# Twelve late modulation units: from TensorE's strips alone to TensorE's strips and VectorE in turn, with the last four placed in the output projection

## The chip, the cores and the metric

The kernel runs on one core of one Trainium2 chip. The metric is device time in microseconds (us) of one execution; the median of several executions is compared. A profile shows one execution, with each engine's instructions: TensorE (PE, matmuls; PEld, its weight loads), VectorE (DVE), ScalarE (ACT), GpSimd (POOL) and SyncE (SP, whose queue issues all loads and stores of this kernel).

## The reference, cut to what matters

Two transformer-like blocks on 256 tokens of width 2048, in fp32. The first block is modulated by a vector `c`:

```python
mod = silu(c) @ ada_w + ada_b                      # ada_w: 2048 x 12288
sh_m, sc_m, g_m, sh_f, sc_f, g_f = split(mod + ada_table, 6)
h = rms(x, norm_mix_pre) * (1 + sc_m) + sh_m
y = rwkv7_mix(h)                                   # projections, a scan over chunks, output projection w_o
x = x + g_m * rms(y, norm_mix_post)
h = rms(x, norm_ffn_pre) * (1 + sc_f) + sh_f
x = x + g_f * rms(conv_ffn(h), norm_ffn_post)
```

The second block (attention and short convolution) is not touched. What matters here is the product `silu(c) @ ada_w`: one row times a matrix of 96 MB. Of its six segments of 2048 columns, the first two (shift and scale ahead of the mixer) are wanted at once. Segments 2 (gate after the mixer), 4 (scale) and 3 (shift ahead of the feed-forward) are wanted only after the output projection, and segment 5 (gate of the feed-forward) at the end of the feed-forward.

## The kernel before, in words

*Units.* A modulation unit is 512 columns of one segment. It loads its 2048 rows as 8 tiles `raw` of 512 KB (two row blocks of 128 each) through SP's queue and adds up 16 products of a row block with 128 values of `silu(c)`. There are two ways to do that:

- `ada_group_pe` (its loads on line 250, its matmuls on line 256): TensorE multiplies a block of 32 columns, of which one holds the values, with the 512 columns. The block number modulo 4 chooses which 32 partitions of the PSUM bank are written, so four row blocks use four strips of the array. At the end ScalarE copies the bank to SBUF (line 260).
- `ada_group` (loads on line 220): VectorE multiplies the row block by a value for each partition (line 232 for the first, line 238 with the accumulator added for the other 15), into an SBUF tile `acc0`.

Either way a unit ends with its finish, `ada_fm`: four matmuls by a column of ones add up the partitions (line 273), and one or two small VectorE instructions follow (line 275 on). `ada_run` is a generator that goes through a list of units. A unit has four steps of two loads each; its finish is called `ADALAG` steps into the next unit, or with `ADALAG = 0` at the beginning of the step after its last.

*Stages.* First the value, key and low-rank projections with segments 0 and 1 (to about 295 us). Then four quarters of four head pairs each (295 to 740 us): `operands` prepares a pair, with its receptance projection `w_r` on TensorE and three stops, and between the stops the code places steps of the previous quarter's `scan` (`SSTEP` of them) and of the late units (`QSTEP` of them). The twelve late units are here: segment 2 (0 to 3), segment 4 (4 to 7), segment 3 (8 to 11), all through `ada_group_pe`, in 16 x 3 = 48 steps. A scan has a triangular inverse (lines 715 to 742, nearly all on VectorE) and then four chunks (lines 784 to 823). The last quarter's scan follows (740 to 830 us), together with a small projection `e_proj` whose evictions use the same `raw` tiles as the units; then the output projection `w_o` in four blocks of 512 columns (`tm_units`, lines 165 to 167, then `tm_out`, which evicts a block), the residual and `to_fm` (900 to 925 us), and the input of the feed-forward in 86 units of `fm_unit` (925 to 1430 us). Beside that run the four units of segment 5, written there in the code, on VectorE.

*Order.* The kernel is built with a framework whose planner lays down each engine's queue when the kernel is built. It takes what the code has earliest among what it reckons to be ready, by its own reckoning of times; the engine then runs its queue strictly in that order. Thus an instruction can stand in a queue ahead of its place in the code, as far as its tiles are free.

*Buffers.* Tiles `raw` of the units have three buffers after 295 us (`NADA2`). The accumulator `acc0` has two, in a pool `accp` that is opened in the feed-forward. The load `l2` of the low-rank weights of a pair has two.

Of the kernel before, what the change touches and what calls it, by code (L numbers as in the profile page):

```python
# [17 lines left out]
NADA = 5  # L18
NADA2 = 3

SSTEP, QSTEP = 3, 1
XL = 4
VST, WST, WP = (2, 2, 2, 2), (0, 0, 0, 0), 2
TAIL = 3
# [1 line left out]

SH = (9999, 9999)
PARTS = ((0, 25), (25, 32))
ADALAG = 2

GROUPS = ((0, 2), (2, 4), (6, 4), (10, 4), (14, 2))
P = 128
# [26 lines left out]
def body(tc, A, out):  # L59
# [5 lines left out]
    def pool(name, bufs=1, **kw):  # L65
        return tc.tile_pool(name=name, bufs=bufs, **kw)
# [146 lines left out]
    def ada_group(seg, k0, nk, accs):  # L213
# [4 lines left out]
        for q in range(KT // n):  # L218
            raw = t_(adap[0], [P, 1024], "raw").rearrange("p (a c) -> p a c", c=w_)
            SP.dma_start(raw, A["ada_w"][q * n * P:(q + 1) * n * P, c0:c0 + w_].rearrange("(a p) c -> p a c", p=P))  # L220
            for a in range(n):
                b = q * n + a
                sc = sil[:, b:b + 1]
                w = 1 if b % 4 < ada_pool[0] else 0
                if accs[w] is None:
                    accs[w] = t_(accp[0], [P, 512], f"acc{w}", bufs=2 - w)
                acc = accs[w][:, :w_]
                if first[w]:
                    if w:
                        S.activation(acc, raw[:, a, :], AF.Copy, scale=sc)  # L230
                    else:
                        V.tensor_scalar(acc, raw[:, a, :], sc, None, op0=ALU.mult)
                elif w:
                    tp = t_(small, [P, 512], "nbr", bufs=1)[:, :w_]
                    S.activation(tp, raw[:, a, :], AF.Copy, scale=sc)
                    G.tensor_tensor(acc, acc, tp, op=ALU.add)
                else:
                    V.scalar_tensor_tensor(acc, raw[:, a, :], sc, acc, op0=ALU.mult, op1=ALU.add)
                first[w] = False
            if q % 2:  # L240
                yield
# [119 lines left out]
    def mix(m, k0, nk, dst, d0=0):  # L361

        mt = t_(pa, [P, 4, T], "mt", bufs=2)[:, :nk, :]
        for i in range(nk):
# [12 lines left out]
    kd = drm.tile([NPAIR, P, T], F32, tag="kd", name="kd")  # L377
    ada_how[0] = ada_group_pe
    adag = [ada_run(0, ada_scale(1, k0, nk, D_AM, V_NPRE), ada_shift(0, k0, nk, D_BM)) for k0, nk in GROUPS]
    ada = ada_run(ADALAG, *[ada_row(2, k0, 4, V_NMP, gmd) for k0 in range(0, KT, 4)],  # L380
                  *[ada_scale(4, k0, 4, D_AF, V_NFP) for k0 in range(0, KT, 4)],
                  *[ada_shift(3, k0, 4, D_BF) for k0 in range(0, KT, 4)])
    xv = t_(hilo, [P, 2, 2, 4, T], "xl", F32R)
    vac = t_(hilo, [P, 2, D], "xh")
    kac = t_(pa, [P, NPAIR, T], "kac")
# [141 lines left out]
    whl[0] = whl_x.enter_context(pool("whlr", NWHL, reuse_waits="tile"))  # L527
    adx = ExitStack()
    adap[0] = adx.enter_context(pool("adap2", NADA2, side="right"))
    phb = ExitStack()  # L530
    pb = phb.enter_context(pool("pb", 2, side="right", reuse_waits="tile"))
    pc_ = phb.enter_context(pool("scan", 1, side="right", reuse_waits="tile"))
# [14 lines left out]
    def operands(j, AR, BK, EC):  # L547

        w, i = divmod(j, 4)
        l2 = t_(pr, [P, 4, P], "l2", bufs=2)  # L550
        SP.dma_start(l2, A["w_l2"][j].rearrange("p (a c) -> p a c", c=P))
        l2h = t_(pr, [P, 4, P], "l2h", F32R)
        l2l = t_(pr, [P, 4, P], "l2l", F32R)
# [297 lines left out]
    for q in range(4):  # L851
# [1 line left out]
        BK = t_(pb, [P, 4, 4, P], "BK")  # L853
        EC = t_(pb, [P, 4, 4], "EC")
        for i in range(4):
            for _ in operands(q * 4 + i, AR, BK, EC):
                for _ in range(SSTEP):
                    next(sc, None)
                for _ in range(QSTEP):
                    next(ada, None)  # L860
        for _ in sc:
            pass
        sc = scan(q, AR, BK, EC)
    for _ in ada:
        pass
    wide_m[0] = True
    phr.close()
    whl_x.close()
# [112 lines left out]
    for nb in range(4):  # L981
# [13 lines left out]
        elif nb == 1:  # L995
            V.tensor_copy(xt[:, 0, 0:1], accs(1)[0][:, 0:1])
            SP.dma_start(xt, A["x"].rearrange("(h p) d -> p h d", p=P))
        tm_out(po, accs(nb), nb, y2, grow, ssq)
    s2 = add_residual(po, y2, ssq, xt)
    for hf in range(2):  # L1000
# [8 lines left out]

    phf = ExitStack()  # L1010
    pf = phf.enter_context(pool("pf", 1, reuse_waits="tile"))
    accp[0] = phf.enter_context(pool("accp", 2, reuse_waits="tile"))
    ada_how[0] = ada_group
    ff = (t_(pf, [P, NFF, T], "ffh", F32R), t_(pf, [P, NFF, T], "ffl", F32R))
    ada = ada_run(ADALAG, *[ada_row(5, k0, 4, V_NFPO, gfd) for k0 in range(0, KT, 4)])
# [407 lines left out]
```

## Time and profile before

| | us |
|---|---|
| median of 3 runs | 2219.46 (2217.79 to 2228.51) |
| profiled execution | 2202.98, span from first to last instruction 2201.2 |
| TensorE busy | 2054.0 (93%) |
| VectorE busy | 1312.3 (60%) |
| ScalarE busy | 1001.7 (46%) |
| loads and stores | 446.36 MB, 203 GB/s over the span |

Busy time is the union of an engine's instructions. In the views by stage each engine has its busy us in the window and the count of its instructions, then PEclk, the clock granted to TensorE (1.00 is 2.4 GHz and 0.5 is 1.2 GHz, so a mean between them is a mixture), the mean busy share of the 16 DMA engines, and the rate.

### The profile page before, as it was taken

How to read it: one execution, taken by the hardware profiler on the slowest of the kernel's cores; microseconds unless marked ns; L12 is line 12 of the kernel's file. 1: busy time of each engine (PE TensorE's matmuls, PEld its weight loads, DVE VectorE, ACT ScalarE, POOL GpSimd, SP SyncE). 2: the span in 40 equal slices, each digit the busy share in tenths (PEclk: the TensorE clock that was granted, in tenths of full speed). 3: DMA queues.
4: the chain of work that ended last, by engine and by line, in shares of the span. 5: the costliest groups of instructions: out<-in, count | busy, mean ns of one | idle time of the engine just before them, and what ended most of it. 6: DMA issues, size and time to landing. Idle time of an engine off the chain costs nothing.

```text
span 2201.2 us, 37566 instructions
## 1 busy us (share of the span) xinstructions
PE 2054.0 (93%) x15092; PEld 1728.1 (79%) x15092; DVE 1312.3 (60%) x2229; ACT 1001.7 (46%) x1554; POOL 387.7 (18%) x210
## 2 busy tenths in 40 slices
PE   6999977699999899799999999999998999999998
PEld 3778854466666467699999999978886889998887
DVE  3687873757676657866567676523336476665435
ACT  3544462234343444545544545434445444454453
POOL 1000000000000000122223222222332322322232
PEclk8999998889999989899999999999999999999999
DMA  8888656777664748665667566576664545556664
GB/s 291 297 297 283 206 199 205 200 200 217 197 209 152 207 150 303 212 193 180 185 183 248 181 213 190 175 233 193 191 196 135 177 144 175 170 165 219 191 197 153
DMA packets 192351, 446.36 MB, mean 203 GB/s; under 512 B 42792, under 2 KB 65448, under 8 KB 190896
## 3 DMA queue, kind: packets, MB, share of 16 engines
q1 hardware_dynamic: 192176, 443.96, 63.9%
q8 instruction: 118, 1.93, 0.4%
q14 instruction: 57, 0.47, 0.1%
HBM read 427.63 MB, written 16.27 MB: 202 GB/s over the span
## 4 chain that ended last, share of the span: by engine, by line
PE 81%; DMA 8%; DVE 6%; ACT 3%; issue 1%; SPq 0%; another core or an unknown queue 0%; POOL 0%; ACTq 0%; DVEq 0%; POOLq 0%
PE ps_s L150 6%; PE ps_s L152 6%; PE ps_s L151 6%; PE ps_g L150 5%; PE ps_g L152 5%; PE ps_g L151 5%; PE ps_a L256 4%; DMA raw<-in_ada_w 4%; PE ps_s L165 4%; PE ps_g L167 4%; PE ps_s L166 4%; PE ps_s L167 4%; PE ps_g L166 4%; PE ps_g L165 4%; DVE wlo L139 1%; PE ps_s L438 1%
## 5 line engine op out<-in xcount | busy, mean ns | idle before, releaser
L135 ACT ACTIVATE whi<-raw 128x1024 fp32r<-128x1024 f32 x562 | 594.0, 1058 | 741.7 <-issue 157.9
L139 DVE TENSOR_TENSOR wlo<-raw,whi 128x1024 fp32r<-128x1024 f32 x414 | 509.7, 1233 | 457.0 <-ACT whi L135 454.2
L139 POOL TENSOR_TENSOR wlo<-raw,whi 128x1024 fp32r<-128x1024 f32 x148 | 363.1, 2454 | 980.6 <-ACT whi L135 944.9
L150 PE MATMUL ps_g<-xh,whi 128*128 128x256 f32 x816 | 236.8, 290 | 14.7 <-ACT whi L135 14.7
L152 PE MATMUL ps_g<-xh,wlo 128*128 128x256 f32 x816 | 236.8, 290 | 3.0 <-DVE wlo L139 2.9
L151 PE MATMUL ps_g<-xl,whi 128*128 128x256 f32 x816 | 236.0, 289 | 0.0
L152 PE MATMUL ps_s<-xh,wlo 128*128 128x256 f32 x816 | 231.1, 283 | 2.7 <-DVE wlo L139 2.7
L150 PE MATMUL ps_s<-xh,whi 128*128 128x256 f32 x816 | 231.1, 283 | 0.0
L151 PE MATMUL ps_s<-xl,whi 128*128 128x256 f32 x816 | 230.9, 283 | 0.0
L150 PEld LDWEIGHTS ps_g<-xh,whi 128*128 128x128 f32 x816 | 160.5, 197 | 26.3 <-ACT whi L135 16.7
L256 PE MATMUL ps_a<-raw,sil 128*32 128x512 f32 (+1 forms) x704 | 139.7, 591 | 36.5 <-DMA raw<-in_ada_w 26.6
L152 PEld LDWEIGHTS ps_g<-xh,wlo 128*128 128x128 f32 x816 | 160.2, 196 | 13.0 <-issue 6.2
L151 PEld LDWEIGHTS ps_g<-xl,whi 128*128 128x128 f32 x816 | 160.4, 197 | 5.0 <-issue 4.2
L152 PEld LDWEIGHTS ps_s<-xh,wlo 128*128 128x128 f32 x816 | 156.6, 192 | 3.1 <-DVE wlo L139 3.1
L150 PEld LDWEIGHTS ps_s<-xh,whi 128*128 128x128 f32 x816 | 156.8, 192 | 0.0
L151 PEld LDWEIGHTS ps_s<-xl,whi 128*128 128x128 f32 x816 | 156.6, 192 | 0.0
L150 PE MATMUL ps_s<-h3h,whi 128*128 128x256 f32 x384 | 107.8, 281 | 0.0
L152 PE MATMUL ps_s<-h3h,wlo 128*128 128x256 f32 x384 | 106.6, 278 | 0.0
L151 PE MATMUL ps_s<-h3l,whi 128*128 128x256 f32 x384 | 106.2, 277 | 0.0
L256 PEld LDWEIGHTS ps_a<-raw,sil 128*32 128x32 f32 x704 | 23.3, 110 | 82.2 <-DMA raw<-in_ada_w 41.1
L150 PEld LDWEIGHTS ps_s<-h3h,whi 128*128 128x128 f32 x384 | 72.2, 188 | 3.6 <-issue 3.5
L152 PEld LDWEIGHTS ps_s<-h3h,wlo 128*128 128x128 f32 x384 | 72.3, 188 | 0.3 <-issue 0.3
(494 smaller groups left out, 4633.0 us busy)
## 6 DMA issues: line engine op xcount, KB each, us to landing
raw<-in_w_f SPq DMA_DIRECT2D x258, 512.0 KB, 4.5
raw<-in_ada_w SPq DMA_DIRECT2D x192, 512.0 KB, 5.4
raw<-in_w_i2f SPq DMA_DIRECT2D x80, 512.0 KB, 3.7
raw<-in_w_o SPq DMA_DIRECT2D x64, 512.0 KB, 4.8
raw<-in_w_v SPq DMA_DIRECT2D x32, 512.0 KB, 4.7
raw<-in_w_k SPq DMA_DIRECT2D x32, 512.0 KB, 4.8
raw<-in_w_r SPq DMA_DIRECT2D x32, 512.0 KB, 7.3
raw<-in_w_g SPq DMA_DIRECT2D x32, 512.0 KB, 4.8
```

The lines of the kernel that those rows point to most:

```text
L135: S.activation(hi, raw, AF.Copy)
L139: e.tensor_sub(lo, raw, hi)
L150: mm(acc, wh[:, sl], xh[:, kt, :], start=(kt == 0), stop=False)
L151: mm(acc, wh[:, sl], xl[:, kt, :], start=False, stop=False)
L152: mm(acc, wl[:, sl], xh[:, kt, :], start=False, stop=(kt == KT - 1))
L165: mm(a, xh, wh[:, sl], start=st, stop=False)
L166: mm(a, xl, wh[:, sl], start=False, stop=False)
L167: mm(a, xh, wl[:, sl], start=False, stop=sp_)
L256: mm(acc[r:r + 32, :w_], sil32[:, b, :], raw[:, a, :], start=(b < 4), stop=(b >= KT - 4))
L438: mm(acc[:, o], wl[:, sl], x[0][:, kt, :], start=False, stop=(i == 1 and kt == nk - 1))
```

## The change

`ON_PE` chooses the units that stay on TensorE: 1, 3, 5 and 7. Units 0, 2, 4 and 6 go through `ada_group` on VectorE. Units 0 to 7 now have all 32 steps of the projections and scans: two for a pair (`QSTEP = 2`, at the first two of the three stops) in place of three. Units 8 to 11 (segment 3) also go through `ada_group`, in 16 steps in the output projection: 4, 6 and 6 steps between the matmuls of blocks 0, 1 and 2 and the eviction of that block (`OSTEP`); the last finish is called in `to_fm`, at the first columns that need it (`LATE`, there before). The finish is no longer lagged. The accumulator's pool is opened earlier and has one buffer in place of two; the low-rank load has one in place of two.

```diff
-SSTEP, QSTEP = 3, 1
+SSTEP, QSTEP = 3, 2
+OSTEP = (4, 6, 6, 0)
+ON_PE = (1, 3, 5, 7)
...
-ADALAG = 2
+ADALAG = 0
...
-                    accs[w] = t_(accp[0], [P, 512], f"acc{w}", bufs=2 - w)
+                    accs[w] = t_(accp[0], [P, 512], f"acc{w}", bufs=1)
...
-    ada = ada_run(ADALAG, *[ada_row(2, k0, 4, V_NMP, gmd) for k0 in range(0, KT, 4)],
-                  *[ada_scale(4, k0, 4, D_AF, V_NFP) for k0 in range(0, KT, 4)],
-                  *[ada_shift(3, k0, 4, D_BF) for k0 in range(0, KT, 4)])
+    late = []
+    for u in range(12):
+        ada_how[0] = ada_group_pe if u in ON_PE else ada_group
+        k0 = u % 4 * 4
+        late.append(ada_row(2, k0, 4, V_NMP, gmd) if u < 4 else ada_scale(4, k0, 4, D_AF, V_NFP) if u < 8
+                    else ada_shift(3, k0, 4, D_BF))
+    ada = ada_run(ADALAG, *late)
...
+    accp[0] = adx.enter_context(pool("accp", 1, side="right"))
...
-        l2 = t_(pr, [P, 4, P], "l2", bufs=2)
+        l2 = t_(pr, [P, 4, P], "l2")
...
-            for _ in operands(q * 4 + i, AR, BK, EC):
+            for e, _ in enumerate(operands(q * 4 + i, AR, BK, EC)):
                 for _ in range(SSTEP):
                     next(sc, None)
-                for _ in range(QSTEP):
+                if e < QSTEP:
                     next(ada, None)
...
-    for _ in ada:
-        pass
...
+        for _ in range(OSTEP[nb]):
+            next(ada, None)
         tm_out(po, accs(nb), nb, y2, grow, ssq)
...
-    accp[0] = phf.enter_context(pool("accp", 2, reuse_waits="tile"))
```

## Rows read from the trace of the kernel before

**Rows 1.** The page, part 1: busy time, share, instructions.
```profile
span 2201.2 us, 37566 instructions
...
PE 2054.0 (93%) x15092; PEld 1728.1 (79%) x15092; DVE 1312.3 (60%) x2229; ACT 1001.7 (46%) x1554; POOL 387.7 (18%) x210
```

**Rows 2.** Windows by stage: window, its us, busy us of each engine.
```profile
295.00:385.00 90.00, 65.53 (x400) 43.32 (x398) 40.34 (x72) 33.37 (x64) 1.89 (x9) 0.87 0.71 220
385.00:500.00 115.00, 92.20 (x991) 64.17 (x993) 69.12 (x195) 39.60 (x81) 2.47 (x8) 0.87 0.76 205
500.00:610.00 110.00, 105.26 (x1125) 72.28 (x1121) 76.17 (x215) 45.59 (x94) 3.13 (x10) 0.97 0.67 204
610.00:740.00 130.00, 123.51 (x1345) 83.79 (x1341) 83.17 (x231) 52.75 (x109) 4.11 (x12) 0.97 0.60 179
740.00:815.00 75.00, 63.81 (x559) 41.92 (x554) 52.45 (x150) 34.26 (x65) 1.19 (x3) 0.89 0.63 191
...
850.00:900.00 50.00, 48.70 (x214) 39.69 (x212) 34.40 (x38) 20.41 (x27) 2.16 (x1) 1.00 0.91 322
900.00:925.00 25.00, 9.90 (x62) 9.24 (x63) 22.57 (x41) 16.33 (x39) 5.93 (x3) 0.66 0.60 204
925.00:1430.00 505.00, 499.80 (x4148) 498.36 (x4147) 320.33 (x417) 250.22 (x348) 139.05 (x57) 1.00 0.62 192
```

**Rows 3.** Windows of line 256 alone: TensorE's matmuls, its weight loads.
```profile
500.00:610.00 110.00, 25.87 (x96) 3.75 (x96) 0.97 0.67 204
610.00:740.00 130.00, 32.29 (x116) 4.51 (x116) 0.97 0.60 179
sum 445.00, PE 98.24 PEld 13.92; mean PE 24.56 PEld 3.48
```

**Rows 4.** The chain of waits from 295 to 740 us, shares by line.
```profile
by line: PE ps_a L256 15.9%; DMA raw<-in_ada_w 9.4%; PE ps_g L152 6.3%; PE ps_g L150 6.2%; PE ps_g L151 6.0%; DMA raw<-in_w_r 4.7%; PE ps_m L636 3.2%; PE ps_s L561 2.5%; PE ps_m L273 2.1%; PE ps_g L808 1.8%; PE ps_s L563 1.8%; PE ps_m L665 
```

**Rows 5.** Windows of 20 us in the scans, columns as in rows 2.
```profile
410.00:430.00 20.00, 19.05 (x134) 12.80 (x133) 19.25 (x86) 5.60 (x9) 0.11 (x1) 0.95 0.87 262
430.00:450.00 20.00, 11.02 (x60) 7.82 (x58) 13.37 (x41) 3.56 (x10) 0.00 (x0) 0.74 0.82 192
...
590.00:610.00 20.00, 20.00 (x259) 14.52 (x258) 9.86 (x21) 9.55 (x19) 0.63 (x2) 1.00 0.50 139
...
650.00:670.00 20.00, 16.89 (x85) 7.90 (x85) 17.52 (x82) 5.95 (x14) 0.00 (x0) 0.91 0.80 251
```

**Rows 6.** The tile `acc`: duration ns min/median/max, first and last start us.
```profile
L238 DVE SCALAR_TENSOR_TENSOR acc<-raw,sil,acc x60: 642/749/2901, 826.5 to 1312.0; 128x512 f32<-128x512 f32 x60
...
L232 DVE TENSOR_SCALAR acc<-raw,sil x4: 477/480/485, 826.0 to 1283.5; 128x512 f32<-128x512 f32 x4
```

**Rows 7.** The tile `raw`, SP's queue: loads of units on VectorE.
```profile
L220 SPq DMA_DIRECT2D raw<-in_ada_w x32: 367/386/876, 773.0 to 1302.4; - x32
```

**Rows 8.** DMA issues of 740:815, 815:900, 900:925 us: KB each, us to landing.
```profile
raw<-in_ada_w SPq DMA_DIRECT2D x3, 512.0 KB, 6.0
...
raw<-in_ada_w SPq DMA_DIRECT2D x14, 512.0 KB, 5.9
...
raw<-in_ada_w SPq DMA_DIRECT2D x2, 512.0 KB, 7.2
```

**Rows 9.** Windows of VectorE's instructions on `acc` alone.
```profile
815.00:900.00 85.00, 22.92 (x30) 1.00 0.79 271
900.00:925.00 25.00, 2.39 (x3) 0.66 0.60 204
```

**Rows 10.** The chain of waits near the end of the residual: start us, us, what.
```profile
909.17 0.72 DVE acc L238
910.00 1.43 DVE xt L910 x2
```

**Rows 11.** Windows in the feed-forward's input, columns as in rows 2.
```profile
1130.00:1170.00 40.00, 37.54 (x312) 37.13 (x311) 32.45 (x44) 15.90 (x23) 10.71 (x4) 1.00 0.75 234
1270.00:1310.00 40.00, 37.26 (x309) 36.85 (x308) 30.62 (x42) 16.86 (x23) 11.22 (x5) 1.00 0.68 215
```

**Rows 12.** Who waited for whom, VectorE, 295 to 740 us: us, times, longest.
```profile
DVE adav L275 <- PE ps_m L273: 11.2, 5, 4.2
...
DVE dv L275 <- PE ps_m L273: 8.5, 3, 3.9
```

**Rows 13.** Who waited for whom, SP's queue, 300 to 740 us.
```profile
SPq L250 <- PE ps_a L256: 115.2, 50, 8.5
```

## The prediction

> **What bounds the kernel now.** I read the page first: TensorE is busy for 93% of the span, so the question is where it is truly the bound, and whether the units' matmuls are on its path [rows 1]. Then the windows, one for each stage. During the projections and scans, 295 to 740 us, TensorE's share grows: 65.5 of 90 us and 92.2 of 115 us in the first two quarters, then 105.3 of 110 and 123.5 of 130. Together that is 386.5 of 445 us, with VectorE at 268.8 [rows 2]. From 740 to 815 us the last scan runs almost alone and every engine has room. The output projection is nearly all TensorE (48.7 of 50 us from 850 on), with DMA at a share of 0.91. From 900 to 925 us VectorE is the bound (22.6 of 25 us), and in the feed-forward input TensorE again (499.8 of 505 us) [rows 2].
>
> The view of line 256 alone says what the twelve late units cost TensorE: 98.24 us, all between 295 and 740 us, or 8.2 us for a unit; the last quarter holds 32.3 us of it [rows 3]. The chain of waits over the same 445 us says that these are not fill: 15.9% of it is line 256 and 9.4% is waiting for its loads, so 70.8 and 41.8 us [rows 4]. That is the room for a gain.
>
> Slices of 20 us show what stands next. In the stretch in which a scan's triangular inverse runs, VectorE is at 17.5 to 19.3 us of 20; there are five such slices (410, 530, 550, 630 and 650 us; the first and last are shown), 100 us of the 445. In the stretch of the chunks (590 us) TensorE has 20.0 of 20 and VectorE 9.9 [rows 5].
>
> **The change part by part.** *Eight units leave TensorE's strips.* Four (0, 2, 4, 6) go to VectorE beside the scans, four (8 to 11) to VectorE after them. 8 x 8.2 = 65.5 us of TensorE work goes. By the chain, two thirds of (70.8 + 41.8) is 75 us, which is the upper bound of the gain in these 445 us.
>
> *VectorE gets four units there.* Each is one product of 0.48 us and 15 multiply-adds of 0.749 us [rows 6], so 11.7 us, 46.9 for four; VectorE goes from 268.8 to 315.7 us. Where TensorE is the bound this is free, covered by VectorE's idle half; in the five full slices it is not. Spread evenly, 100/445 of it, 10.5 us, would fall there; all 46.9 on the path is the other end. I take a third, 16 us, since loads also arrive late for VectorE, whose queue holds the scan's next step behind them.
>
> *TensorE is less dense.* Its work would be 321 us of about 395, or 81%. The quarter at 80% (385 to 500 us) had a granted clock of 0.87, those at 95% 0.97 [rows 2], and the half-idle slice at 430 us 0.74 [rows 5]. If the last two quarters fell to 0.87, the 190 us of work left in them (228.8 less two thirds of their 25.9 + 32.3 on line 256 [rows 3]) would grow by 0.10/0.87, 22 us; zero if the gaps stay short. I take 9, as TensorE is not always the bound any more. The Trainium skill (TensorE: Matmul & The Clock Gate, "Why this matters for your kernels") warns of idle gaps between bursts of matmuls, after which the clock is back at the lower level; the slice at 430 us agrees (0.74), and by this rule alone the 22 us would be paid.
>
> The scans' stage thus gains 75 - 16 - 9 = 50 us, between 6 (75 - 47 - 22) and 75.
>
> *Units 8 to 11 in the projection.* They are 32 loads of 512 KB and 64 VectorE instructions. The stretch is not empty before: the planner has already put there the feed-forward gate's units, which the code has much later. 19 of their 32 loads are issued from 773 to 925 us [rows 7, 8], and 22.92 + 2.39 us of their VectorE work lies there [rows 9]. The new units come first in the code, so they displace these. The surplus is 13 loads, 6.8 MB, and 46.9 - 25.3 = 21.6 us of VectorE. At the best rate shown, 322 GB/s [rows 2], the bytes are 21 us. From below: between 740 and 815 us DMA moves 191 GB/s and VectorE idles 22.5 us, so both fit and the cost is 0, if unit 8 is pulled into that stretch. Another way: with three buffers the units' loads ran at 445/96 = 4.6 us each beside the scans; 32 from 773 us on end at 920 us, against 910 us for the last accumulation before the residual now [rows 10]. I take 11 us.
>
> *The gate's units move back.* Two more then run inside the feed-forward input. Around each of the two there now TensorE idles 2.5 and 2.7 us of 40 [rows 11]. So 5 us; zero if VectorE's 185 idle us hide them.
>
> *Finish without lag, one accumulator, one low-rank buffer.* The finishing matmuls are as many as before. With no lag they are asked for one step after the last accumulation, not three; VectorE waited 11.2 and 8.5 us for them in 445 us [rows 12], and TensorE can now wait for VectorE's sum: between nothing and one late load (5.9 us [rows 8]) for each of four units, 24 us. I take 2, as a step of other work lies between. In the projection two such finishes stand inside one batch; that is in the second rival. The single low-rank buffer costs nothing: the next pair's load stands in SP's queue behind this pair's last store, long after the buffer was read.
>
> The sum: -50 + 11 + 5 + 2 = -32 us. The profiled execution took 2202.98 us, and would take 2171. The median of the runs is 2219.46, 0.7% above it, and I forecast against that: 2187 us.
>
> **The rivals.** *VectorE becomes the bound of the scans.* For it: the five full slices. Against: they are under a quarter of the stage. Then all 46.9 us count: 75 - 47 - 9 = 19 gained, 18 paid, 2218 us, no change.
>
> *Slower: units 8 to 11 come late.* They share one accumulator, so each waits for TensorE to finish the one before it, and their loads go through three buffers on SP's queue, which stood 115.2 us for such buffers beside the scans [rows 13]. The feed-forward input needs their sums. The gate's units began to accumulate at 826 us and took 17 loads in 83 us, 5 us each [rows 6, 10]. At that start and pace 32 loads end near 986 us, 76 after now: -50 + 76 + 7 = +33 us, 2252 us. It decides from an end of about 953 us, that is, a start after 790 us at 5.1 us a load. Against it: the gate's units came last in the code and got what was left; these come before the work that they stand beside, and loads began at 773 us.
>
> *The clock falls wherever TensorE has gaps.* 22 us instead of 9: 2200 us. It is the page's rule above; for it speaks 0.74 at 430 us, against it 0.91 at 650 us, where TensorE is busy 16.9 of 20 us [rows 5].
>
> *Nothing takes the place of what goes.* 75 - 16 in the scans, the projection's extra in the gaps of the last scan, 2 for the finishes: -57, 2162 us. For it: DMA and VectorE are both below two thirds and three quarters before 815 us.
>
> That the units don't leave is no case: the diff changes the engine by construction.
>
> **How the numbers follow.** Forecast 0.52, own range 2168 to 2207 (one of its terms at its bound). VectorE-bound 0.14, late units 0.14, clock 0.08, full gain 0.12. The likeliest gives 2187. The range 2152 to 2226 takes in all but the late units' larger prices and the last few us of the full gain, under 2 in 10. A measurement of this kernel tells about 0.5%, 11 us, from no change. Faster: 0.52 + 0.08 + 0.12 = 0.72; same 0.14; slower 0.14.
>
> **What would show it.** Line 256 falls from 98 to about 33 us beside the scans, and the wait for its loads to a third. Lines 232 and 238 appear there with 64 instructions and 47 us. Stage by stage: the last scan's first matmuls near 690 us instead of 739; from there to the end of the residual some 10 us more than now; the gate's units all after that, and the feed-forward input 5 us longer. The slices of the inverse show VectorE at 9 tenths or more, TensorE below 8. I am wrong if the scans' stage shrinks by under 25 us, with VectorE's queue standing for the units' loads, or if TensorE stands between blocks of the output projection, waiting for weights whose loads are queued behind the units'.

## The result, and the profile after

The changed kernel took 2231.29 us (median of 19 runs, 2223.4 to 2249.77), the kernel before 2218.59 us on the same chips (19 runs, 2210.74 to 2228.51). The ratio is 1.0075, with a 95% interval of 1.0053 to 1.0096: slower, by a little more than a measurement of this kernel can tell from no change. The forecast was 2187 us, faster.

The profiled execution of the changed kernel took 2223.5 us, 20.5 us more than that of before. The medians differ by 12.7 us: the profiled execution of before (2202.98 us) was shorter than any of its 19 runs here, so some 8 us of the 20.5 belong to the two executions that were profiled. This is part 1 of its page, to be read beside [rows 1].

```profile
span 2221.7 us, 37226 instructions
...
PE 2029.7 (91%) x14836; PEld 1746.2 (79%) x14836; DVE 1399.7 (63%) x2357; ACT 998.0 (45%) x1546; POOL 389.7 (18%) x210
```

TensorE is busy for 24 us less, VectorE for 87 us more. So work did move, and the span still grew. Where it grew is read stage by stage, from the first starts of four lines. The first transpose of a triangular inverse (tile `NT`) ends the first quarter; the last one starts the last scan. The residual's first product (`y`, line 935, 929 before) ends the projection, and the last `u` product ends the input of the feed-forward. For the changed kernel these are the rows by line (columns as in [rows 6]: duration ns min/median/max, first and last start in us):

```profile
L701 DVE STREAM_TRANSPOSE NT<-TQ x4: 1897/1972/1992, 379.5 to 713.0; 64x1024 f32<-64x1024 f32 x4
...
L935 DVE TENSOR_SCALAR y<-xt,rsx x8: 477/480/487, 917.2 to 920.3; 128x512 f32<-128x512 f32 x8
...
L1045 DVE TENSOR_TENSOR u<-u,u x43: 414/425/1247, 944.4 to 1443.5; 128x256 f32<-128x256 f32 x43
```

For the kernel before the same four marks are 400.2, 741.5, 913.6 and 1429.1 us. The differences between marks give this table, and the same reading gives the stages of every experiment further on:

| stage, us | before | after | change | forecast |
|---|---|---|---|---|
| start to the end of the first quarter | 400.2 | 379.5 | -20.7 | -50 with the next row |
| the other three quarters | 341.3 | 333.5 | -7.8 | |
| last scan, output projection, residual | 172.1 | 204.2 | +32.1 | +11, and +2 for the finishes |
| input of the feed-forward | 515.5 | 526.3 | +10.8 | +5 |
| the rest | 772.1 | 778.2 | +6.1 | 0 |
| sum | 2201.2 | 2221.7 | +20.5 | -32 |

The scans gained 28.5 us and the projection lost 32.1. How far one execution can be trusted is seen from seven kernels of this document that differ only behind the quarters (the changed one, and those of the experiments on units 8 to 11, unit 7's finish, the two accumulators, loads, work, and the gate's units). Their first quarter ends at 379.5 to 388.8 us, and the other three take 331.0 to 340.8 us. So two single executions tell less than 10 us in either stage from nothing, and the 7.8 us of the second row are not clear of that. The changed kernel's profiled execution has the shortest quarters of the seven: against this one execution of before, the scans' gain lies between 12 and 28.5 us.

The windows by stage show how it came, beside [rows 2]:

```profile
295.00:380.00 85.00, 62.11 (x494) 46.50 (x494) 58.12 (x104) 39.70 (x76) 2.30 (x10) 0.90 0.79 233
380.00:490.00 110.00, 86.57 (x879) 69.52 (x878) 83.18 (x220) 40.43 (x82) 3.01 (x9) 0.82 0.71 188
490.00:600.00 110.00, 93.60 (x1151) 74.17 (x1147) 90.23 (x237) 47.02 (x97) 3.23 (x11) 0.89 0.62 184
600.00:711.00 111.00, 95.72 (x1025) 72.45 (x1026) 74.07 (x211) 41.38 (x87) 3.01 (x9) 0.86 0.34 100
...
850.00:900.00 50.00, 39.65 (x147) 30.73 (x148) 35.73 (x43) 15.14 (x17) 0.00 (x0) 0.86 0.83 283
900.00:930.00 30.00, 15.24 (x86) 13.60 (x85) 23.25 (x39) 17.36 (x40) 7.87 (x3) 0.72 0.51 181
930.00:1445.00 515.00, 501.88 (x4152) 499.35 (x4152) 344.38 (x450) 250.95 (x351) 141.71 (x57) 1.00 0.65 205
```

Beside the scans TensorE's share has gone from about 95% to 85% in the last two quarters, and the granted clock from 0.97 to 0.89 and 0.86. From 850 to 900 us, in the midst of the output projection, TensorE is busy for 39.65 of 50 us, where it had 48.70. That is new.

The 20 us slices, to be read beside [rows 5], show what the scans wait for now:

```profile
395.00:415.00 20.00, 10.41 (x52) 7.49 (x48) 18.29 (x75) 5.73 (x12) 0.11 (x1) 0.72 0.61 165
415.00:435.00 20.00, 13.05 (x171) 12.04 (x171) 19.95 (x41) 5.01 (x9) 0.11 (x1) 0.69 0.51 163
...
515.00:535.00 20.00, 7.88 (x35) 6.67 (x34) 19.99 (x82) 4.24 (x11) 0.00 (x0) 0.53 0.29 82
```

Before, TensorE did 19.05 and 16.89 us of work in the slices of an inverse at 410 and 650 us, the units' matmuls (6.33 and 9.57 us) among it. Now VectorE is full for the whole slice and TensorE has little to do; at 515 us it works 7.88 of 20 us and the granted clock is 0.53. So the units' matmuls had stood in the gaps that the inverse leaves to TensorE.

In the projection the chain of waits in order of time (start, duration, link) names two loads of `w_o` on TensorE's path. Each is issued right behind a load of a unit (line 223), which had waited for VectorE's multiply-add. The finish of the last late unit stands after the residual has begun:

```profile
836.23 1.09 PE ps_m L276 x8
...
837.98 0.98 issue
838.95 0.76 DVE acc L241
839.73 0.37 SPq L223
840.15 10.31 DMA raw<-in_w_o
850.55 1.06 ACT whi L138
851.65 0.79 PE ps_g L168
...
880.47 0.37 SPq L223
880.94 6.61 DMA raw<-in_w_o
887.63 1.06 ACT whi L138
...
927.83 0.80 PE ps_m L276 x8
```

Slices of 10 us there show DMA all but stopped from 790 to 810 us and at its best rate from 820 us on; TensorE has holes at 840, 870 and 880 us:

```profile
790.00:800.00 10.00, 8.78 (x101) 6.16 (x97) 3.29 (x9) 3.01 (x8) 0.00 (x0) 0.69 0.12 26
800.00:810.00 10.00, 10.00 (x89) 7.38 (x89) 4.63 (x12) 2.21 (x6) 0.00 (x0) 1.00 0.08 29
...
820.00:830.00 10.00, 10.00 (x46) 8.29 (x45) 8.43 (x11) 5.00 (x8) 0.00 (x0) 1.00 0.92 306
...
840.00:850.00 10.00, 6.70 (x29) 5.20 (x27) 4.09 (x6) 0.00 (x0) 0.00 (x0) 0.97 1.02 384
...
870.00:880.00 10.00, 5.47 (x22) 3.56 (x21) 8.03 (x12) 1.11 (x2) 0.00 (x0) 1.00 0.84 281
880.00:890.00 10.00, 5.87 (x15) 4.41 (x16) 7.32 (x9) 2.93 (x3) 0.00 (x0) 0.75 0.95 331
```

What SP's queue waited for from 705 to 935 us (us in total, times, longest) puts the units' loads first: they stand for their tiles, until VectorE has used them.

```profile
SPq L223 <- DVE acc L241: 38.7, 21, 5.5
SPq L135 <- DVE wlo L142: 18.4, 10, 6.1
...
SPq L1278 <- PE ps_a L276: 12.1, 1, 12.1
```

The lull of DMA from 790 to 810 us has another cause than these waits: there the queue stands 8.0 us for a load of the last scan (line 785) and then 12.1 us for a row tile that unit 7's finish still reads (line 1278). The kernel without units 8 to 11, further on, has the same 12.1 us and 11 GB/s from 800 to 810 us, in a projection stage of 176.8 us. So the lull isn't what the stage lost.

### The profile page after: what moved, and what is told of

It is laid out like the page before. It is cut to its first block, busy times and chain, and to the rows that moved or that the text cites. A ratio compares the mean times of both kernels' runs of the same rounds, so it can differ in the third digit from the quotient of the medians.

```text
span 2221.7 us, 37226 instructions
## 1 busy us (share of the span) xinstructions
PE 2029.7 (91%) x14836; PEld 1746.2 (79%) x14836; DVE 1399.7 (63%) x2357; ACT 998.0 (45%) x1546; POOL 389.7 (18%) x210
## 4 chain that ended last, share of the span: by engine, by line
PE 74%; DMA 11%; DVE 10%; ACT 2%; issue 2%; SPq 0%; POOL 0%; DVEq 0%; ACTq 0%; POOLq 0%
DMA raw<-in_ada_w 6%; PE ps_s L153 6%; PE ps_s L155 6%; PE ps_s L154 5%; PE ps_g L155 5%; PE ps_g L153 5%; PE ps_g L154 5%; PE ps_g L170 4%; PE ps_g L168 4%; PE ps_g L169 4%; PE ps_s L168 4%; PE ps_s L169 4%; PE ps_s L170 3%; PE ps_a L259 2%; DVE acc L241 2%
## 5 line engine op out<-in xcount | busy, mean ns | idle before, releaser
L241 DVE SCALAR_TENSOR_TENSOR acc<-raw,sil,acc 128x512 f32<-128x512 f32 x180 | 156.3, 869 | 27.6 <-DMA raw<-in_ada_w 25.9
L259 PE MATMUL ps_a<-raw,sil 128*32 128x512 f32 (+1 forms) x448 | 77.4, 570 | 20.1 <-DMA raw<-in_ada_w 19.9
L153 PE MATMUL ps_g<-h3h,whi 128*128 128x256 f32 x256 | 72.9, 285 | 0.0
```

The source lines that it names most:

```text
L153: mm(acc, wh[:, sl], xh[:, kt, :], start=(kt == 0), stop=False)
L259: mm(acc[r:r + 32, :w_], sil32[:, b, :], raw[:, a, :], start=(b < 4), stop=(b >= KT - 4))
```

## The experiments

Ratios are to the kernel before on the same chip; stages are from one profiled execution each. Five kernels were run once: they have a single time and no interval.

**The late units 8 to 11 left out.** The first question is whether the projection is the whole loss.

```diff
-    ada = ada_run(ADALAG, *late)
+    ada = ada_run(ADALAG, *late[:8])
```

> Changed kernel with units 8 to 11 left out (the shift ahead of the feed-forward is set to zero): no loads, no VectorE work and no finishes of theirs in the output projection. Theory P (these four units lose the time: 32.6 us between the last scan's first matmul and the residual, and 11 us in the feed-forward's input, where the gate's units were pushed): the former stretch falls from 206 to about 174 us, the gate's units come back into it, and the whole is 30 to 45 us faster than the changed kernel, near 2190 us. Theory S (the units on VectorE beside the scans lose the time): no more than 10 us faster.

Measured: 2207.75 us, ratio 0.9942 (0.9919 to 0.9966). The stage of the projection is 176.8 us in place of 204.2, so the four units cost 27.4 us there. The three quarters stay at 336.9. The gain of the scans is there, and it is small: this kernel leaves out a third of the late units and is still only 11 us faster than the one before. So there are two failures to explain, one in each stage. Theory P came true for the projection and not for the feed-forward's input: of the gate's two units only one came back into the projection (16 instructions there, 32 before), and that input still takes 525.9 us.

**Unit 7's finish at the end of the quarters.** Its finish stands at 805.8 us in the changed kernel, between the end of one unit and the start of the next. Is the late finish what holds units 8 to 11?

```diff
-    ada = ada_run(ADALAG, *late)
+    ada = ada_run(ADALAG, *late[:8])
+    for _ in ada:
+        pass
+    ada = ada_run(ADALAG, *late[8:])
```

> Changed kernel with the finish of unit 7 called at the end of the quarters instead of in the output projection. Theory N (that late finish is what costs: it holds the row tile for which SP's queue stood 12.1 us, and unit 8's finish stands behind it, so that the single accumulator is idle from 780 to 812 us): the stretch from the last scan to the residual falls by 12 to 25 us, the whole by as much. Theory P in its plain form (bytes and VectorE work are too many): within 5 us of the changed kernel.

Measured: 2242.35 us, ratio 1.0091 (1.0056 to 1.0127); the projection's stage is 206.8 us. Nothing was gained. The theory that this finish holds the units up fell.

**Two accumulators for units 8 to 11.** A new pool of two buffers is opened at the end of the quarters, which the gate's units use later too; nothing else differs.

```diff
-                    accs[w] = t_(accp[0], [P, 512], f"acc{w}", bufs=1)
+                    accs[w] = t_(accp[0], [P, 512], f"acc{w}", bufs=accb[0])
...
+    accp[0], accb[0] = accx.enter_context(pool("accp2", 2, reuse_waits="tile")), 2
```

> Changed kernel with two accumulators in place of one from the end of the quarters on, so that a unit's first product need not wait for the finish of the one before. Theory A (the single accumulator holds the units up: it is idle from 780 to 812 us): the stretch falls by 10 to 20 us. If the loads themselves are what stands in the way: within 5 us of the changed kernel, or longer, as more loads are issued ahead of weights.

Measured: 2217.39 us, ratio 1.0010 (0.9988 to 1.0033); the projection's stage is 190.5 us, 13.7 less than with one. The slices at 790 and 840 us show what the second accumulator changes:

```profile
790.00:800.00 10.00, 7.71 (x107) 5.91 (x104) 6.65 (x15) 2.62 (x7) 0.00 (x0) 0.84 0.69 213
...
840.00:850.00 10.00, 10.00 (x46) 8.26 (x45) 5.46 (x6) 3.71 (x6) 0.00 (x0) 1.00 0.96 390
```

DMA now runs at 213 GB/s from 790 us, where it had 26, and TensorE has no hole at 840 us. So the single accumulator is shown to cost about 14 us in this stage. In the changed kernel unit 8's last multiply-add starts at 784.1 us, its finish at 810.3, and only then, at 811.4, unit 9's first product; with two accumulators that product starts at 789.4. SP's queue stands for the units' tiles for 28.0 us in place of 38.7 (705 to 935 us).

**All loads of units 8 to 11, but little work.** The multiply-adds of these units are cut from 512 columns to 8. Beside it the other half: all the work, but one load for each unit, whose tile is used eight times.

```diff
-                    V.scalar_tensor_tensor(acc, raw[:, a, :], sc, acc, op0=ALU.mult, op1=ALU.add)
+                    V.scalar_tensor_tensor(acc[:, :8], raw[:, a, :8], sc, acc[:, :8], op0=ALU.mult, op1=ALU.add)
```

> Units 8 to 11 with all their 32 loads, waits and finishes, but the 60 multiply-adds are cut from 512 to 8 columns (the sums are those of the first row block only, save for 8 columns): VectorE's work on them falls from 47 to some 8 us. Theory Q (SP's queue and the bytes cost: loads of units stand in front of the weights of the output projection): the stretch from the last scan to the residual stays within 8 us of the changed kernel's 204 us. Theory V (VectorE's work delays the weights' splits and the evictions): it falls to 185 us or less.

```diff
-            raw = t_(adap[0], [P, 1024], "raw").rearrange("p (a c) -> p a c", c=w_)
-            SP.dma_start(raw, A["ada_w"][q * n * P:(q + 1) * n * P, c0:c0 + w_].rearrange("(a p) c -> p a c", p=P))
+            if q == 0:
+                raw = t_(adap[0], [P, 1024], "raw").rearrange("p (a c) -> p a c", c=w_)
+                SP.dma_start(raw, A["ada_w"][q * n * P:(q + 1) * n * P, c0:c0 + w_].rearrange("(a p) c -> p a c", p=P))
```

> Units 8 to 11 with all their VectorE work and finishes, but one load for a unit instead of eight (the eight products use the first tile): 4 loads instead of 32 in the output projection. Theory Q: the stretch from the last scan to the residual falls from 204 to 185 us or less. Theory V: within 8 us of the changed kernel.

Measured: loads with little work 2215.18 us, 0.9999 (0.9971 to 1.0027), stage 191.1 us; work with one load 2205.35 us, 0.9960 (0.9936 to 0.9984), stage 180.8 us. Over the 176.8 us without these units (which hold one of the gate's units), the work alone is 4.0 us and the loads alone 14.3 us; together they are 27.4. The remaining 9 us belong to neither alone; that the work holds the tiles, so that the loads hold the queue, is the reading that fits the waits. In the kernel with the loads alone SP's queue still stands for the tiles, from 705 to 935 us:

```profile
SPq L253 <- DVE acc L271: 28.3, 17, 6.9
SPq L253 <- DMA raw<-in_ada_w: 17.6, 8, 6.5
```

**Units 0 to 7 all on TensorE, 8 to 11 as in the change.** This separates the engine of the eight from their number of steps.

```diff
-ON_PE = (1, 3, 5, 7)
+ON_PE = (0, 1, 2, 3, 4, 5, 6, 7)
```

> Projection part alone: units 0 to 7 all on TensorE's strips, 8 to 11 on VectorE in the projection as in the changed kernel. Theory C (the scans' own chain of about 107 us for a quarter sets the stage whatever stands beside it): scans' stage 410 to 420 us as in the changed kernel, projection as long as there, so within 8 us of it. Theory S: without units on VectorE the scans are 12 us or more shorter than in the changed kernel.

Measured: 2233.73 us, ratio 1.0055 (1.0029 to 1.0081), not to be told from the changed kernel. Stages: 382.7, 340.4, 207.6 us. The first quarter has the same gain without VectorE. With all eight on TensorE the other three take 340.4 us, and with four on VectorE 331.0 to 340.8 in seven executions: for eight units the engine makes no difference that these runs can show.

**All twelve units beside the scans, in turn on the two engines,** with three steps for a pair as before, and none in the projection.

```diff
-SSTEP, QSTEP = 3, 2
-OSTEP = (4, 6, 6, 0)
-ON_PE = (1, 3, 5, 7)
+SSTEP, QSTEP = 3, 3
+OSTEP = (0, 0, 0, 0)
+ON_PE = (1, 3, 5, 7, 9, 11)
```

> Scan part alone: all twelve units beside the scans, three steps for a pair, 0, 2, .. 10 on VectorE and 1, 3, .. 11 on TensorE, all finished before the projection. Theory P: projection and feed-forward as in the kernel before (174 us and 516 us), scans' stage 416 to 425 us instead of 445, so 20 to 30 us faster than the kernel before. Theory S (VectorE's six units lengthen the scans): scans' stage 440 us or more, and no faster than the kernel before.

Measured: 2251.66 us, ratio 1.0144 (1.0111 to 1.0177). The first quarter ends at 412.3 us (400.2 before) and the other three take 364.8 (341.3 before); the projection's stage is 177.1. Six units taken from TensorE and given to VectorE make the three quarters 23.5 us longer, not shorter. The theory that the part in the scans gains by itself fell. (This kernel has the finish without lag, the single accumulator and the single low-rank buffer too; what they cost beside the scans was not taken apart.) A 20 us slice in its inverse:

```profile
560.00:580.00 20.00, 9.94 (x45) 7.63 (x43) 20.00 (x80) 3.96 (x9) 0.11 (x1) 0.59 0.25 79
```

VectorE is full, TensorE half idle, the granted clock 0.59.

**None of the twelve units,** to find how short the scans can be.

```diff
-    ada = ada_run(ADALAG, *late)
+    ada = iter(())
```

> Changed kernel with none of the twelve late units (gate, scale and shift after the mixer are set to zero): shows the scans' stage bare. Theory C (the scan's own chain sets the three quarters that hold one): from the first to the last transpose of the inverse still 320 us or more, against 333 in the changed kernel and 341 before. Rival (units on either engine fill it): 300 us or less.

Measured: 2160.3 us (one run). The first quarter ends at 369.6 us and the other three take 303.3 us, 38 less than before. One theory put at least 320 us there, and missed: the bare scans are shorter. The window of the three quarters and the chain of waits in it:

```profile
369.00:673.00 304.00, 252.36 (x2912) 213.85 (x2912) 218.37 (x612) 126.37 (x260) 9.22 (x29) 0.83 0.29 83
```

```profile
by line: DVE XT L742 7.2%; DVE pt L739 7.2%; PE ps_g L153 5.4%; PE ps_g L154 5.4%; PE ps_g L155 5.2%; PE ps_m L649 3.8%; PE ps_m L770 3.5%; PE ps_g L821 3.5%; DVE wlo L142 3.4%; issue 3.3%; PE ps_g L823 3.0%; PE ps_s L626 2.8%; PE ps_s L797
```

Without any unit, TensorE has 52 us of idle time in these three quarters, and the two VectorE lines of the inverse (739 and 742) lead the chain. So behind the chain through TensorE's units stands another that runs in part through VectorE's inverse.

**Work or loads beside the scans.** Both kernels leave units 8 to 11 out, as the first experiment does. One gives each of units 0 to 7 a single load, used eight times; the other has all 64 loads, with the products cut to 8 columns after each accumulation's start.

```diff
-                mm(acc[r:r + 32, :w_], sil32[:, b, :], raw[:, a, :], start=(b < 4), stop=(b >= KT - 4))
+                n8 = w_ if b < 4 else 8
+                mm(acc[r:r + 32, :n8], sil32[:, b, :], raw[:, a, :n8], start=(b < 4), stop=(b >= KT - 4))
```

> The run without units 8 to 11, and units 0 to 7 with one load each instead of eight (the products are all there, of the first tile): the scans have all the work of the eight units and 8 loads instead of 64. Bare scans took 303 us for the three quarters with a scan, eight whole units 337. Theory L (late loads, for which TensorE's and VectorE's queues stand, lengthen the scans): 303 to 315 us. Theory W (the work on the engines does): 325 us or more.

> The run without units 8 to 11, and units 0 to 7 with all 64 loads, waits and finishes, but products cut from 512 to 8 columns save for the first (sums incomplete). Theory L: 325 us or more for the three quarters. Theory W: 303 to 315 us.

Measured (one run each): one load 2193.19 us, three quarters 326.3 us; little work 2174.56 us, three quarters 305.9 us. All loads with little work are 2.6 us above no units at all, all the work with an eighth of the loads 23.0 us above; both together, in the first experiment, 33.6. So the theory of late loads fell for these three quarters, and work is what costs, though loads added to the work bring another 10.6 us, no more than the scatter. In the first quarter, which has no scan, it is rather the other way: it ends at 369.6 us without units, 371.9 with the work and 379.2 with the loads.

**Which engine's work.** Again without units 8 to 11: only TensorE's units (1, 3, 5, 7), then only VectorE's (0, 2, 4, 6), with the other four left out as well (`x if u not in ON_PE` in the second).

```diff
+    late = [x if u in ON_PE else (iter([None] * 4), lambda: None) for u, x in enumerate(late)]
```

> The run without units 8 to 11, with only the four units of TensorE (1, 3, 5, 7) left beside the scans, at the same steps; the other four are left out (their results are zero). Bare 303 us for the three quarters with a scan, all eight 337. If TensorE's units are fill there (VectorE's inverse leaves it idle): 303 to 310 us. If they lengthen the scans as much as VectorE's: about 320 us.

> The same with only the four units of VectorE (0, 2, 4, 6) left. If VectorE is what the scans are bound by (four units there are 47 us of its work in the stage): 325 to 337 us, most of the eight units' price. If both kinds cost alike: about 320 us. If they are fill: 303 to 310 us.

Measured (one run each): TensorE's four 2170.77 us, VectorE's four 2195.03 us. For each, the transposes that mark the three quarters, and the units' own busy time in them. TensorE's four:

```profile
L708 DVE STREAM_TRANSPOSE NT<-TQ x4: 1927/1937/1949, 374.6 to 687.5; 64x1024 f32<-64x1024 f32 x4
```

```profile
374.00:687.00 313.00, 25.28 (x96) 3.46 (x96) 0.87 0.42 122
```

VectorE's four (the fourth busy time here is VectorE's; the first two are the finishes on TensorE):

```profile
L708 DVE STREAM_TRANSPOSE NT<-TQ x4: 1921/1963/1985, 385.8 to 715.9; 64x1024 f32<-64x1024 f32 x4
```

```profile
386.00:716.00 330.00, 3.16 (x24) 2.90 (x24) 30.23 (x42) 0.81 0.40 114
```

The three quarters take 312.9 and 330.1 us, against 303.3 without units. 25.28 us of TensorE's matmuls lengthen them by 9.6 us, 38%; 30.23 us of VectorE's multiply-adds by 26.8 us, 89%. The 17.2 us between the two kernels are more than the scatter of 10 us, the 9.6 us are not. Thus, at four units, a unit costs the scans more on VectorE than on TensorE, though TensorE's matmuls fill more of the time. Two things go with it: with units on TensorE the granted clock is higher (0.87 against 0.81), and in these quarters TensorE's units stand between 387 and 514 us, VectorE's between 391 and 645.

**The gate's units with lag and two accumulators as before,** for the 10.8 us in the feed-forward.

```diff
+    accp[0], accb[0] = phf.enter_context(pool("accpf", 2, reuse_waits="tile")), 2
...
-    ada = ada_run(ADALAG, *[ada_row(5, k0, 4, V_NFPO, gfd) for k0 in range(0, KT, 4)])
+    ada = ada_run(2, *[ada_row(5, k0, 4, V_NFPO, gfd) for k0 in range(0, KT, 4)])
```

> Changed kernel with the gate's units of the feed-forward as they were before: two accumulators in a pool of their own and a finish lagged by two steps. The stretch from the residual to the end of the feed-forward's input was 515.5 us before and 523 to 528 in every variant so far. If the lag and the accumulator cost there: back to 518 us or less, the whole 6 to 10 us faster than the changed kernel. If it is that all four units run there now instead of two: no change beyond 3 us.

Measured: 2242.66 us, ratio 1.0090 (1.0063 to 1.0118), with 525.0 us in the input of the feed-forward, as in the changed kernel (526.3). Lag and accumulators aren't the cause there. The number of the gate's units inside the stage is a candidate, but it doesn't settle it: the stage takes 515.5 and 517.8 us with two of them (before, and the uneven kernel below), 523 to 529 us with three and 523 to 528 us with four. No run took that number alone as its variable.

**The kernel before, with its units spread unevenly over the quarters.** All twelve stay on TensorE; the quarters get 8, 12, 12 and 16 steps in place of 12 each.

```diff
-SSTEP, QSTEP = 3, 1
+SSTEP = 3
+QN = ((1, 1, 0), (1, 1, 1), (1, 1, 1), (2, 1, 1))
```

> Kernel before with all twelve units on TensorE's strips, but 8 of the 48 steps in the first quarter instead of 12, and 12, 12 and 16 in the others. In every variant with two steps for a pair the first quarter was 11 to 21 us shorter than before. If that quarter is bound by its loads and the others have room for four more steps: 8 to 15 us faster than the kernel before. If the other quarters are full: they grow by as much, within 5 us.

Measured: 2214.62 us, ratio 0.9973 (0.9955 to 0.9991). The first quarter ends at 384.5 us, 15.7 earlier; the other three take 358.8, 17.5 longer. Four fewer steps in the first quarter gain about what the change gained there, with no unit on VectorE at all; given back to the last quarter, they cost as much in these two executions. By the medians the kernel is 6 us faster, short of the 8 to 15 of the first theory; so before's one profiled execution makes that price look larger than it is.

**One late unit.** From this follows a kernel: eleven units on TensorE, 8 steps in the first quarter and 12 in each of the others, and only the last unit on VectorE, in the projection. With one unit the single accumulator has nobody waiting for it.

```diff
+QN = ((1, 1, 0), (1, 1, 1), (1, 1, 1), (1, 1, 1))
+OSTEP = (5, 0, 0, 0)
+ON_PE = tuple(range(11))
```

> A version that might beat both: units 0 to 10 on TensorE's strips in 44 steps (8 in the first quarter, 12 in each other), unit 11 alone on VectorE in the output projection, finish without lag. If the projection's loss comes from four units queued one behind the other on one accumulator: one unit costs there 3 us or less, and the quarters gain those four steps, so 5 to 15 us faster than the kernel before. If a single unit's loads already hold the weights up: no faster than the kernel before.

Measured: 2203.77 us (2193.29 to 2209.41, 8 runs), ratio 0.9925 (0.9895 to 0.9955): faster than both kernels. Stages: 377.9, 339.4, 178.1 and 523.4 us. The projection's stage is 1.3 us above that without units 8 to 11, and 6.0 us above before's. Its scans' windows:

```profile
490.00:605.00 115.00, 105.21 (x1138) 74.20 (x1137) 77.93 (x219) 52.55 (x104) 3.13 (x10) 0.99 0.66 197
605.00:717.00 112.00, 107.23 (x1265) 75.72 (x1264) 80.57 (x224) 49.30 (x100) 3.13 (x10) 0.98 0.62 186
```

TensorE is again at 91 to 96% of these windows, at a granted clock of 0.98 to 0.99.

## Why the prediction was wrong, point by point

**The step that failed first** is "By the chain, two thirds of (70.8 + 41.8) is 75 us", taken as what comes back when eight units leave TensorE. The shares were read rightly: 15.9 and 9.4% of the chain of waits did run through line 256 and its loads [rows 4]. What they are worth was not. The kernel with units 1, 3, 5 and 7 alone is close to this step by itself (one run): its last scan starts at 687.5 us, 54.0 us earlier than before, and not 75. Even all twelve units are worth 68.6 us (30.6 in the first quarter and 38.0 in the other three), where the chain had 112.6 us running through them. Without the units the chain goes another way, with two lines of the inverse on VectorE as the largest. The step also let two thirds of the waits for loads go, while 64 of the 96 loads stay beside the scans. In the changed kernel's chain from 295 to 711 us these waits are 10.0% of 416 us, 41.6 us as before; the matmuls fell to 24.1 us, a third, as forecast:

```profile
by line: DMA raw<-in_ada_w 10.0%; PE ps_g L155 7.5%; PE ps_g L153 7.2%; PE ps_g L154 6.8%; PE ps_a L259 5.8%; PE ps_m L644 4.5%; DVE XT L737 3.4%; DVE pt L734 3.3%; DVE acc L241 2.9%; PE ps_s L569 2.6%; issue 2.4%; PE ps_s L621 2.3%; PE ps_
```

The Trainium skill (Perfetto Trace Analysis, "Identifying the Most-Contended Engine") says to judge TensorE's headroom by MFU (the share of its peak rate that a kernel reaches) and by the busy share of its weight loads, not by that of its matmuls. By weight loads TensorE stood at 156.07 of 240 us in the last two quarters, 65%, and VectorE was busy for 159.34, 66% [rows 2]; without units the two are 213.85 and 218.37 of 304 us. So by this measure there was no engine with much more room than the other.

The work itself was counted rightly. Line 259 now has 36 us beside the scans (33 forecast) and VectorE's units have 46.3 (47 forecast); in the second row below the third busy time is VectorE's:

```profile
sum 416.00, PE 36.06 PEld 4.82; mean PE 12.02 PEld 1.61
```

```profile
295.00:711.00 416.00, 4.21 (x32) 3.87 (x32) 46.26 (x64) 0.86 0.60 173
```

**"I take a third, 16 us", for VectorE's part.** The four units on VectorE put the last scan's start from 687.5 us (TensorE's four alone) to 713.0, so 25.5 us with what the clock cost, against 16 + 9 forecast; in the other six executions of these quarters it was 29 to 42 us. So this term was about right or too small, and the larger part of the scans' miss lies in the 75. Without TensorE's units beside them, 26.8 of 30.23 us fell on the path, 89%, near the other end of the stated bounds. The first rival, VectorE as the bound of the scans, described that case, and my slices had shown it [rows 5]; I weighed five full slices of 20 us as a quarter of the stage. That work put on VectorE in an inverse delays the whole quarter, since the rest of the quarter follows it, is my reading; no run moved the units within a quarter.

**What the scans gained is mostly another thing.** 20.7 of the 28.5 us came in the first quarter, which has no scan beside it. There the units had 12 steps and now have 8. The uneven kernel, with these eight on TensorE, gains 15.7 us there, and the kernel with one late unit 22.3. These differ by less than the scatter of single executions. So it is the number of steps that counts in this quarter, not the engine; the two kernels that take loads and work apart there point to the loads. My sum had no term for the first quarter by itself.

**The clock, 9 us.** Its direction was right: the granted clock of the last two quarters fell from 0.97 to 0.89 and 0.86. Its price is read from the same matmuls before (500 to 740 us) and after (490 to 711 us). For one line of `w_r` (busy us, mean ns):

```profile
L151 PE MATMUL ps_g<-xl,whi 128*128 128x256 f32 x144 | 43.0, 298 | 0.0
```

```profile
L154 PE MATMUL ps_g<-xl,whi 128*128 128x256 f32 x128 | 38.5, 301 | 0.0
```

The other two lines of `w_r` go from 297 and 294 to 307 and 306 ns, and all matmuls that both windows have are 3.7% longer on the mean, weighted by their time. Of 189 us busy that is some 7 us (an estimate from these means): near the 9, far from the 22 of the bound. So a fall of the mean granted clock by a tenth did not make TensorE's matmuls a tenth longer. The rule of the Trainium skill cited in the prediction (TensorE: Matmul & The Clock Gate, "Why this matters for your kernels") agrees with the slice at 515 us, 7.88 busy us of 20 at 0.53; the 22 us that I drew from it were not paid.

**The projection, "I take 11 us".** It cost 32.1 us with the finishes. My mechanism, surplus loads and work that displace the gate's units, holds: the gate's 60 multiply-adds after the first of each unit all stand from 932 us on now, against 30 from 1142 us. But the price was set by the second rival's things: of the 27.4 us that the four units cost, loads alone are 14 us, work alone 4, and what they do to each other 9. One accumulator accounts for 14 us (shown); this is another cut of the same 27.4 us and not to be added. The other 4.7 us of the 32.1 are there without units 8 to 11 too, and have no cause found. The rival itself was too dear. The last unit's finish stands at 928 us, while its loads alone were to end at 986: unit 8 did run in the last scan, and the loads came at up to 384 GB/s once the queue moved. "I am wrong ... if TensorE stands between blocks of the output projection, waiting for weights whose loads are queued behind the units'": that is what the chain at 840 and 881 us shows.

**The finishes, 2 us.** In the scans they cost no more than before: line 276 is on the chain from 295 to 711 us seven times, with 7.3 us in all (1.00 + 1.79 + 0.98 + 0.80 + 0.98 + 0.79 + 0.98), and line 273 had 2.1% of 445, 9.3 us [rows 4]. In the projection they are part of the accumulator's 14 us, which I had put in a rival.

**The input of the feed-forward, 5 us.** 10.8; the direction was right, the term mis-sized. I had reckoned two stalls of 2.5 us, one for each displaced unit [rows 11]. From 930 us on TensorE's waits for the low half of weights that VectorE makes (`wlo`) grew from 5.2 us to 12.5. Before:

```profile
PE ps_s L152 <- DVE wlo L139: 2.7, 2, 1.9
PE ps_g L152 <- DVE wlo L139: 2.5, 2, 2.0
```

After:

```profile
PE ps_s L155 <- DVE wlo L142: 8.0, 4, 2.6
PE ps_g L155 <- DVE wlo L142: 4.5, 3, 2.0
```

That is 7.3 of the 10.8 us. What makes VectorE late there stays open: the waits are 11.4 us with three of the gate's units in the stage, too.

**The single low-rank buffer, nothing.** The reason was wrong: the next pair's load did wait for the buffer, 14.8 us in four waits of SP's queue (line 559, 295 to 713 us; 2.1 us in one before). What that cost, no run shows.

**One rival's argument** was misread from the rows: "DMA and VectorE are both below two thirds and three quarters before 815 us" isn't so for DMA, whose share is 0.71, 0.76 and 0.67 in the first three quarters [rows 2].

**The rest of the kernel** is 6.1 us longer, though nothing in it was changed. It is 781 us in the uneven kernel, whose code from there on is that of before (772.1), and 775 to 781 in all other kernels that were run. So it belongs to the execution, not to the change.

**What stays open.** The price of a unit on TensorE beside the scans isn't linear. The three quarters take 303 us with none, 313 with 12 steps on TensorE (four units, of which three fall there), 340 with 24, and 339 to 341 with 36, in one execution each. The traces say in part why 24 steps cost as much as 36. TensorE is busy just as long, 303.0 of 340 us with 24 and 302.1 of 339 us with 36 (the kernel with one late unit), though its units' matmuls are 52.9 and 72.4 us of that; the granted clock is 0.88 and 0.95, and the same matmuls are 6% longer with 24. Why the clock is lower there, and what the single accumulator and the single low-rank buffer cost beside the scans, no run shows.

## What to carry to other kernels

A share of the chain of waits is not a gain. Here 112.6 us of the chain ran through the units, all of them together were worth 68.6, and eight of them 54: ask how long the stage would be without that work at all, and which chain then leads. The engine with the lower busy share isn't always the cheaper place for fill: the first four units cost these scans less (in one run each) on TensorE, which idles in the serial inverse, than on VectorE, which runs it; for eight units the place made no difference that could be seen. And where a group of loads goes through few tiles on a queue that also carries the next stage's weights, a second accumulator can be worth as much as the bytes (14 us each here): see what lets go of each tile, and what stands in the queue behind it.

## What the runs showed that I had not expected

Late loads beside the scans are almost free if little work hangs on them: 64 loads of 512 KB in these four quarters, with the products cut to 8 columns, left the last three at 305.9 us against 303.3 without them, at 171 GB/s in place of 83; the first quarter, without a scan, ended 9.6 us later. And with four units on one engine alone, a multiply-add of VectorE cost the scans 0.89 us for each us that it took, where a us of TensorE's matmuls cost 0.38, although in the same quarters without units VectorE is busy for 72% of the time and TensorE for 83%.
